# Residual input and final output of a two-layer trunk turned by VectorE's 32x32 transposes and by the transfers, with matmul tiles of every second column

## The chip, the cores and the metric

The kernel runs on one core of a Trainium2 chip. The metric is the device time of one execution in microseconds (us); the figure for the kernel before is the median of its runs. Inputs and outputs are in DRAM, so every load and store counts.

## The reference

One inference step of two layers on 1024 prompt tokens and 8 single decode tokens, in fp32, feature width 1024. What matters here is how the residual runs through it:

```python
def retention_layer(x, S0, g_norm, w_in, g_out, w_out):
    h = rmsnorm(x, g_norm)
    proj = h @ w_in                      # q, k, v, gate
    ...
    o, S = retention_scan(q, k, v, S0)   # 4 heads, 8 chunks of 128 tokens
    o = rmsnorm(o, g_out) * silu(gate)
    return x + o @ w_out, S              # w_out: 2048 x 1024
```

The second layer has the same frame: `h = rmsnorm(x, g)`, a projection to q, k, v and a gate, attention over a window of 128 tokens (16 query heads, 2 key heads, with sinks) in place of the scan, and `x + o @ w_out` with a 1024 x 1024 `w_out_swa`. The results are `y_prompt`, `y_sample` and the new states and caches.

## The kernel before, in words

All activations between the layers lie with features on the 128 partitions and tokens along the free dimension: 1032 token columns, in which columns 1024 to 1031 are the decode tokens. A matrix product takes 128 features of the output at a time, as a PSUM tile of 128 features by up to 512 tokens. Every fp32 operand is split into a high and a low part, so that each product of a 128-row weight block is three matmuls: high times high, high times low, low times high.

The input x and the output y lie in DRAM the other way, with tokens as rows. So x, as it is loaded for the residual, has to be turned, and so has y before it is stored. Before, TensorE does this: `tr` (L100, L101 in the profile) is a matmul against the identity.

The work around the change, in order of time:

- **The scan** (up to about 695 us). It computes the retention. During its last steps the first output tile of `w_out_ret` is already worked on: `b_w` (L1026) loads 128 columns of the weight in four pieces on SP's queue, `b_wc` (L1032) splits them on ScalarE (L1039) and VectorE (L1040), `b_x` (L1043) loads the matching piece of x, `b_wmm` (L1047) multiplies (L1055 to L1057), and four transposes (L1107, L1108) add the residual into the same PSUM tile, named S. In these steps the loads lie in a ring of buffers named evp, evx, evc, evw.
- **The output projection of the retention layer**, called ro here (about 695 to 835 us). It goes by output tiles (ft, gi): ft is one of 8 blocks of 128 features, gi one of the token ranges RG = 0 to 512, 512 to 768, 768 to 1032. First all eight ft of gi 0, then for every ft the ranges gi 1 and 2. The weights come in slots (`wslot`, L1137): 1024 rows by 256 columns, loaded in two halves of 512 KB (L1144, SP's queue, tile wr with two buffers), and split by ScalarE (L1147, tile wh) and VectorE (L1148, tile wl) with the gain of the norm; a slot therefore serves the two neighbouring ft. `ro_ahead` (L1189) issues slots in advance. `ro_part` (L1197) holds the matmuls L1214 to L1216. `ro_xr` (L1222) loads the x of one tile (L1226, L1229). `ro_finish` (L1231) closes a tile: TensorE's transposes add the residual in PSUM (L1241, L1243, in the profile L101 `pj<-ident,xr`), ScalarE copies the sum out (L1250) and writes the next layer's operands from PSUM (L1252), VectorE their low part (L1253), ScalarE squares (L1258), and the sum goes to the DRAM buffer xscr (L1260, ScalarE's queue). At the border of the scan and ro the order is written out (L1281 to L1285): `ro_ahead(2)`, `ro_finish(0, 0)`, then `ro_xr` of the next two tiles.
- **The second layer's projections and attention** (about 835 to 1225 us), with weights of `w_in_swa` through the same `wslot`.
- **The output projection of the second layer**, called so here (its last part runs alone to the end). `so_all` (L1788) goes over tiles (ft, ti), ti one of the token ranges 0 to 384, 384 to 768, 768 to 1032; VectorE adds the residual from xscr (L1813, tile sq), and `so_y` (L1771), one tile late, turns the sum with three transposes (L1777, L1779, in the profile L101 `tr<-ident,sq`), ScalarE copies it out of PSUM (L1781, L1785) and issues the stores (L1782, L1786). The last two feature blocks (ft 6 and 7) stand at the end, ft by ft. Slots of `w_out_swa` are split in blocks of 128x512 (L1154 on ScalarE, L1157 on VectorE). Between the tiles of this last part the decode tokens' attention is finished: L1725 puts its probabilities on a block diagonal, L1737 and L1739 multiply with the values.

In the scan, and where `manual_schedule` stands, each engine's instructions are in the order of the code; elsewhere a scheduler orders them. SP and ScalarE issue their DMAs in order: an issue that has to wait holds back all that stands behind it on its queue.

Of the kernel before, what the change touches and what calls it, by code (L numbers as in the profile page):

```python
# [20 lines left out]
DV = 512  # L21
# [49 lines left out]
def _trunk(ctx, tc, nc, a):  # L71
# [334 lines left out]
    gl = sp.tile([25, 128], F32, name="gl")  # L406
    rT = sp.tile([128, 7, 4, 4], F32, name="rT")
# [213 lines left out]
    def gains():  # L621
        pg = vdp.tile([128, 512], F32, tag="vd", name="pg")
        tr(pg[:, :25], gl, ident[:25, :25])
        heads[0]["pg"] = pg

    def small_loads():
        for o_, src in ((gl[0:16], ret_out_norm.rearrange("o (k p) -> (o k) p", p=128)),
                        (gl[16:24], norm_swa.rearrange("o (k p) -> (o k) p", p=128)),
                        (gl[24:25, 0:64], q_norm), (gl[24:25, 64:128], q_norm)):
            nc.scalar.dma_start(out=o_, in_=src)  # L630
    later(5, small_loads)
    later(14, gains)
    later(15, lambda: act(gcol, heads[0].pop("pg")[:, :25], AF.Copy))
# [392 lines left out]
    def b_w(i):  # L1026

        t = ring("px"[i // 2])[:, 0:512].rearrange("p (k f) -> p k f", k=4)
        nc.sync.dma_start(out=t, in_=w_out_ret[i * 512:i * 512 + 512, 0:128].rearrange("(k p) f -> p k f", p=128))
        wo[i] = t  # L1030

    def b_wc(i):  # L1032

        raw = wo[i]
        hi, lo = [(woh[i + 2 * (x == "l")] if i < 2 else rp.tile([128, DV], F32R, tag="v" + x, name="wo" + x, bufs=2))
                  .rearrange("p (k f) -> p k f", k=4) for x in "hl"]
        for k in range(4):
            gk = gcol[:, 4 * i + k:4 * i + k + 1]
            act(hi[:, k], raw[:, k], AF.Copy, scale=gk)  # L1039
            dve.scalar_tensor_tensor(lo[:, k], raw[:, k], gk, hi.bitcast(F32)[:, k], MUL, SUB)  # L1040
        wo[i] = hi, lo

    def b_x():  # L1043
        wo["x"] = ring("c")[:, 0:512].rearrange("p (c f) -> p c f", c=4)
        nc.sync.dma_start(out=wo["x"], in_=x_prompt[0, 0:512, 0:128].rearrange("(c p) f -> p c f", p=128))

    def b_wmm(i):  # L1047
# [3 lines left out]
        hi, lo = wo[i]  # L1051
        xh, xl, _ = o_view(0)
        for k in range(4):
# [3 lines left out]
            mm(wo["ps"], lo[:, k, :], xh[:, kt, 0:512], start=False, stop=False)  # L1057
# [20 lines left out]
    for i in range(-1, NS + 2):  # L1078
# [8 lines left out]
        if i in (NS - 3, NS - 2):  # L1087
            b_w(i - NS + 3)
        if i in (NS - 2, NS - 1):
            b_w(i - NS + 4)  # L1090
        if i == NS - 1:
            b_x()
# [911 lines left out]
```

## Time and profile before

| | us |
|---|---|
| median of 3 runs | 1313.86 |
| the runs | 1311.10 to 1314.79 |
| the profiled execution | 1314.25 |
| its span, first to last instruction | 1312.2 |
| TensorE (PE) busy | 1284.0 (98%) |
| VectorE (DVE) busy | 727.7 (55%) |
| ScalarE (ACT) busy | 691.4 (53%) |
| GpSimd (POOL) busy | 630.8 (48%) |

The transfers move 193.98 MB in 199907 packets, and the granted TensorE clock is 0.995 of full speed on average. A row of the timeline reads: start in us, duration in us, engine, line, operation, out<-in, shape, count, and in brackets the idle time before it with what ended it. PE's matmuls overlap in a pipeline, so what one costs is read from the distance between starts, not from its duration. SPq and ACTq are DMA issues on the queues of SyncE and ScalarE. In the grouped rows stand, behind the bar, busy time and mean duration in ns, then idle time ahead of the group with its releasers; in the rows of waits, the time in all, how often, and the longest. A row of windows gives, for a stretch of time, each engine's busy time, the granted clock, the DMA engines' busy share and GB/s.

### The profile page before, as it was taken

How to read it: one execution, taken by the hardware profiler on the slowest of the kernel's cores; microseconds unless marked ns; L12 is line 12 of the kernel's file. 1: busy time of each engine (PE TensorE's matmuls, PEld its weight loads, DVE VectorE, ACT ScalarE, POOL GpSimd, SP SyncE). 2: the span in 40 equal slices, each digit the busy share in tenths (PEclk: the TensorE clock that was granted, in tenths of full speed). 3: DMA queues.
4: the chain of work that ended last, by engine and by line, in shares of the span. 5: the costliest groups of instructions: out<-in, count | busy, mean ns of one | idle time of the engine just before them, and what ended most of it. 6: DMA issues, size and time to landing. Idle time of an engine off the chain costs nothing.

```text
span 1312.2 us, 26102 instructions
## 1 busy us (share of the span) xinstructions
PE 1284.0 (98%) x9597; PEld 1212.2 (92%) x9597; DVE 727.7 (55%) x1476; ACT 691.4 (53%) x1722; POOL 630.8 (48%) x800
## 2 busy tenths in 40 slices
PE   6999999999999999999999999999999999999998
PEld 6999999999999999887887889999999999998998
DVE  6944556565565564477785333324665666766321
ACT  5533544554555653577775444445576666666121
POOL 6654544545445544599980110137476676554000
PEclk9999999999999999999999999999998999999999
DMA  6314767677676854456556554353032211237232
GB/s 225 104 61 129 238 197 244 180 234 220 197 239 184 247 174 138 132 169 213 177 165 193 162 165 123 122 147 85 17 106 72 65 58 44 75 110 251 73 96 78
DMA packets 199907, 193.98 MB, mean 148 GB/s; under 512 B 12916, under 2 KB 180140, under 8 KB 199764
## 3 DMA queue, kind: packets, MB, share of 16 engines
q1 hardware_dynamic: 165024, 157.78, 39.2%
q10 hardware_dynamic: 34756, 34.53, 8.3%
q8 instruction: 76, 1.25, 0.4%
q14 instruction: 51, 0.42, 0.1%
HBM read 132.23 MB, written 61.08 MB: 147 GB/s over the span
## 4 chain that ended last, share of the span: by engine, by line
PE 91%; DVE 2%; ACT 2%; DMA 2%; POOL 2%; issue 1%; ACTq 0%; SPq 0%; POOLq 0%; DVEq 0%
PE b L331 7%; PE b L332 7%; PE b L333 7%; PE pj L1167 6%; PE pj L1168 6%; PE pj L1169 6%; PE tr L101 4%; PE b L324 4%; PE b L325 4%; PE b L326 4%; PE pj L1214 4%; PE pj L1215 4%; PE pj L1216 4%; PE o L1645 2%; PE b L538 2%; PE sc L1610 1%
## 5 line engine op out<-in xcount | busy, mean ns | idle before, releaser
L331 PE MATMUL b<-xh,woh 128*128 128x258 f32 x784 | 223.2, 285 | 0.0
L333 PE MATMUL b<-xh,wol 128*128 128x258 f32 x784 | 221.7, 283 | 0.0
L332 PE MATMUL b<-xl,woh 128*128 128x258 f32 x784 | 221.6, 283 | 0.0
L1167 PE MATMUL pj<-A_hi,wh 128*128 128x384 f32 (+1 forms) x512 | 174.9, 342 | 1.7 <-ACT A_hi L1670 1.3
L1168 PE MATMUL pj<-A_lo,wh 128*128 128x384 f32 (+1 forms) x512 | 165.2, 323 | 0.1
L1169 PE MATMUL pj<-A_hi,wl 128*128 128x384 f32 (+1 forms) x512 | 165.1, 322 | 0.0
L331 PEld LDWEIGHTS b<-xh,woh 128*128 128x128 f32 x784 | 148.0, 189 | 4.1 <-issue 3.7
L332 PEld LDWEIGHTS b<-xl,woh 128*128 128x128 f32 x784 | 148.7, 190 | 0.0
L333 PEld LDWEIGHTS b<-xh,wol 128*128 128x128 f32 x784 | 148.0, 189 | 0.0
L222 POOL TENSOR_TENSOR wol<-raw,woh 128x512 fp32r<-128x512 f32 x52 | 68.1, 1318 | 130.9 <-ACT woh L217 128.8
L324 PE MATMUL b<-woh,xh 128*128 128x256 f32 x448 | 126.6, 283 | 0.0
L325 PE MATMUL b<-wol,xh 128*128 128x256 f32 x448 | 126.0, 281 | 0.0
L326 PE MATMUL b<-woh,xl 128*128 128x256 f32 x448 | 125.6, 280 | 0.0
L1167 PEld LDWEIGHTS pj<-A_hi,wh 128*128 128x128 f32 x512 | 97.3, 190 | 5.4 <-issue 2.6
L1168 PEld LDWEIGHTS pj<-A_lo,wh 128*128 128x128 f32 x512 | 97.5, 190 | 0.4 <-DVE A_lo L1671 0.4
L1169 PEld LDWEIGHTS pj<-A_hi,wl 128*128 128x128 f32 x512 | 96.9, 189 | 0.0
L1148 DVE SCALAR_TENSOR_TENSOR wl<-wr,gcol,wh 128x256 fp32r<-128x256 f32 x128 | 53.8, 486 | 68.2 <-ACT wh L1147 68.2
L1259 POOL TENSOR_TENSOR acc<-acc,sq 128x256 f32<-128x256 f32 (+1 forms) x28 | 20.6, 742 | 146.4 <-ACT sq L1258 146.3
L1625 POOL TENSOR_TENSOR s<-s,sm 128x512 f32<-128x512 f32 x64 | 66.5, 1039 | 47.7 <-DVE sm L1624 43.5
L324 PEld LDWEIGHTS b<-woh,xh 128*128 128x128 f32 x448 | 84.3, 188 | 5.0 <-issue 2.9
L326 PEld LDWEIGHTS b<-woh,xl 128*128 128x128 f32 x448 | 84.3, 188 | 0.0
L325 PEld LDWEIGHTS b<-wol,xh 128*128 128x128 f32 x448 | 84.3, 188 | 0.0
(391 smaller groups left out, 3636.6 us busy)
## 6 DMA issues: line engine op xcount, KB each, us to landing
raw<-in_w_in_ret_dram ACTq DMA_DIRECT2D x44, 512.0 KB
st<-in_state_ret_dram SPq DMA_DIRECT2D x64, 256.0 KB
out_dram<-st SPq DMA_DIRECT2D x64, 256.0 KB
wr<-in_w_out_ret_dram SPq DMA_DIRECT2D x32, 512.0 KB
wr<-in_w_in_swa_dram SPq DMA_DIRECT2D x18, 512.0 KB
vb<-vscr SPq DMA_DIRECT2D x64, 128.0 KB
evp<-qks SPq DMA_DIRECT2D x32, 256.0 KB
evx<-vsc SPq DMA_DIRECT2D x32, 256.0 KB
```

The lines of the kernel that those rows point to most:

```text
L222: eng.tensor_tensor(lo, src_of(s, name, sub), hi.bitcast(F32), SUB)
L324: mm(dst, xh, wh, start=a and i == 0, stop=False, skip_group_check=True)
L325: mm(dst, xh, wl, start=False, stop=False, skip_group_check=True)
L326: mm(dst, xl, wh, start=False, stop=z, skip_group_check=True)
L331: mm(dst, wh, xh, start=a, stop=False, **sg)
L332: mm(dst, wh, xl, start=False, stop=False, **sg)
L333: mm(dst, wl, xh, start=False, stop=z, **sg)
L1148: nc.vector.scalar_tensor_tensor(lo[:, k, :], raw[:, k % 4, :], gk, hi.bitcast(F32)[:, k, :], ALU.mult, ALU.subtract)
L1167: mm(ps, hi[:, k, fs], xh[:, k, t0:t1], start=first and k == ks[0], stop=False)
L1168: mm(ps, hi[:, k, fs], xl[:, k, t0:t1], start=False, stop=False)
L1169: mm(ps, lo[:, k, fs], xh[:, k, t0:t1], start=False, stop=last and k == ks[-1])
L1625: nc.gpsimd.tensor_tensor(st[:, :, 0:256], st[:, :, 0:256], sm.unsqueeze(2).broadcast_to([128, 2, 256]), ALU.mult)
```

## The change

TensorE no longer turns the residual or the output. VectorE has a transpose that turns each 32x32 block of a tile in its place; the transfers put the blocks where they belong. A block row of 32 partitions then holds, in DRAM, runs of 64 features (256 bytes) of one token, so that a load of x for 256 features and 256 tokens is four DMAs of 32 partitions. Since such a tile carries 64 features in a row for each group of 32 partitions, a matmul tile takes every second column of a block of 256: the even ones are ft = 2p, the odd ones 2p + 1. All that depends on the order of features follows: the slots of both output weights are split with a stride of two columns, the rows of `w_in_swa` are loaded in pairs (`rows_load`, two DMAs of 256 KB for one of 512 KB), and the gain of the second norm is turned in the new order (`gs`, two small transposes on TensorE early in the kernel).

- In ro, `ro_finish` takes a VectorE transpose of the loaded x and a VectorE addition of PSUM and x in place of the PE transposes and the ScalarE copy; the operations behind it read SBUF, not PSUM. The decode tokens' x is loaded and turned once (`ro_xd`).
- In the scan, `b_x` and its four transposes are gone; `b_w` loads 256 rows by 256 columns in eight pieces and uses every second column.
- At the border of scan and ro, `ro_xr` for the first two pieces (eight DMAs) now stands ahead of `ro_ahead(2)`.
- In so, `so_y` is a VectorE transpose into a tile that two neighbouring ft share; after the second of them four DMAs store it (four more for the decode tokens). The two last ft go range by range, so that pairs end together. Slots of `w_out_swa` are split in eight blocks of 128x256.

The core of the diff:

```diff
-    def b_w(i):
-        t = ring("px"[i // 2])[:, 0:512].rearrange("p (k f) -> p k f", k=4)
-        nc.sync.dma_start(out=t, in_=w_out_ret[i * 512:i * 512 + 512, 0:128].rearrange("(k p) f -> p k f", p=128))
+    def b_w(i, tag):
+        wo[i] = ring(tag)[:, 0:512].rearrange("p (k f) -> p k f", k=2)
+        nc.sync.dma_start(out=wo[i], in_=w_out_ret[i * 256:i * 256 + 256, 0:256].rearrange("(k p) f -> p k f", p=128))
...
-        for n in {NS - 2: (0,), NS - 1: (1, 2), NS: (3,)}.get(i, ()):
+        for n in {NS - 2: (0,), NS - 1: (1, 4, 2, 3, 5), NS: (6, 7)}.get(i, ()):
             b_wc(n)
...
-    for i in range(4):
-        tr(wo["ps"][:, i * 128:i * 128 + 128], wo["x"][:, i, :], ident, start=False, stop=(i == 3))
...
-    def wslot(src, gain=None):
+    def wslot(src, gain=None, out=False):
...
+                h2, l2 = [t[:, k, :].rearrange("p (u q) -> p u q", u=2) for t in (hi, lo)]
+                r2 = raw[:, k % 4, :].rearrange("p (q u) -> p u q", u=2)
+                if gain is not None:
+                    gk = gcol[:, gain + k:gain + k + 1]
+                    nc.scalar.activation(h2, r2, AF.Copy, scale=gk)
+                    nc.vector.scalar_tensor_tensor(l2, r2, gk, h2.bitcast(F32), ALU.mult, ALU.subtract)
+                else:
+                    nc.scalar.activation(h2, r2, AF.Copy)
+                    lo_eng[0].tensor_tensor(l2, r2, h2.bitcast(F32), ALU.subtract)
...
+    def ro_xr(pr, a):
+        xr = ro_x[pr, a] = fp.tile([128, 8, 64], F32, name="xr", bufs=4)
+        v = x_prompt[0, a:a + 256, 256 * pr:256 * pr + 256].rearrange("(a i) (b f) -> b i a f", i=32, b=4)
+        for b in range(4):
+            nc.sync.dma_start(out=xr[32 * b:32 * b + 32], in_=v[b])
...
-            for i in range(nfull):
-                tr(ps[:, i * 128:i * 128 + 128], xr[:, i, :], ident, start=False, stop=(i == nfull - 1))
...
-            nc.scalar.activation(x1[:, :n], pv, AF.Copy)
+            nc.vector.transpose(x1[:, 0:256], xr[:, u])
+            nc.vector.tensor_tensor(x1[:, 0:256], ps[:, a - t0:a - t0 + 256], x1[:, 0:256], ALU.add)
...
     with tc.manual_schedule(engines={ET.Activation, ET.DVE, ET.Pool, ET.SP}):
+        for a_ in (0, 256):
+            ro_xr(0, a_)
         ro_ahead(2)
         ro_finish(0, 0)
-        for ft in (1, 2):
-            ro_xr(ft, 0)
+        ro_xd()
...
-        for i in range(nch):
-            tr(pt[:, i * 128:i * 128 + 128], yt[:, i * 128:i * 128 + 128], ident)
...
+        nc.vector.transpose(yo[:, 0:nb, :, u], yt[:, 0:32 * nb])
+        if u == 1:
+            fs = slice(256 * pr, 256 * pr + 256)
+            v = y_p[0, t0:t0 + npr, fs].rearrange("(a i) (b f) -> b i a f", i=32, b=4)
+            for b in range(4):
+                bs = slice(32 * b, 32 * b + 32)
+                nc.scalar.dma_start(out=v[b], in_=yo[bs, 0:na].rearrange("i a j u -> i a (j u)"))
```

What follows is the order of the instructions on two engines where the prediction speaks of them; it holds no times.

SP's queue at the border of the scan and ro, before. Tiles evp, evx, evc are the ring in which the scan's last loads lie (L1029 are the four loads of `b_w`, L1045 the load of `b_x`), wr are halves of weight slots.

```order
L1029 DMA evp<-in_w_out_ret_dram 128x4x128
L1029 DMA evx<-in_w_out_ret_dram 128x4x128 x2
L1045 DMA evc<-in_x_prompt_dram 128x4x128
L1144 DMA wr<-in_w_out_ret_dram 128x4x256 x4
L1226 DMA xr<-in_x_prompt_dram 128x4x128 x2
```

The same place after (L1038 are the last of the eight loads of `b_w`, L1240 the decode tokens' x).

```order
L1038 DMA evx<-in_w_out_ret_dram 128x2x256
L1038 DMA evc<-in_w_out_ret_dram 128x2x256
L1038 DMA evp<-in_w_out_ret_dram 128x2x256
L1038 DMA evw<-in_w_out_ret_dram 128x2x256
L1249 DMA xr<-in_x_prompt_dram 32x8x64 x8
L1149 DMA wr<-in_w_out_ret_dram 128x4x256 x2
L1249 DMA xr<-in_x_prompt_dram 32x8x64 x2
L1149 DMA wr<-in_w_out_ret_dram 128x4x256 x2
L1240 DMA xd<-in_x_sample_dram 8x4x64 x4
```

The loads of x, which stood behind the first four halves of weight slots, now stand ahead of them.

VectorE in so, where the decode tokens' probabilities are put on their diagonal (L1725), before; tiles sq are the sums with the residual.

```order
L1813 TENSOR_TENSOR sq_15986<-pj_15961,xr2_15959 128x384
L1813 TENSOR_TENSOR sq_16022<-pm_15997,xr2_15995 128x384
L1725 TENSOR_TENSOR pm8_16055<-tr_16056,ident_70 8x128
L1813 TENSOR_TENSOR sq_16071<-pj_16033,xr2_16031 128x384
L1813 TENSOR_TENSOR sq_16124<-pj_16082,xr2_16080 128x384
L1745 TENSOR_TENSOR gdec_78<-gdec_78 128x64
```

The same place after (L1836 are the sums, L1799 the transposes of the output, L1743 is the former L1725).

```order
L1836 TENSOR_TENSOR sq_16052<-pm_16027,xr2_16025 128x384
L1799 STREAM_TRANSPOSE yo_16101<-sq_16052 128x384
L1836 TENSOR_TENSOR sq_16099<-pj_16061,xr2_16059 128x384
L1799 STREAM_TRANSPOSE yo_16101<-sq_16099 128x384
L1836 TENSOR_TENSOR sq_16147<-pj_16105,xr2_16103 128x384
L1743 TENSOR_TENSOR pm8_16083<-tr_16084,ident_70 8x128
L1799 STREAM_TRANSPOSE yo_16183<-sq_16147 128x384
L1763 TENSOR_TENSOR gdec_78<-gdec_78 128x64
```

Before, two sums stood between the diagonal and what is done with the decode tokens' attention (L1745, now L1763); now the diagonal stands behind both.

VectorE in so, where the low parts wl of the last slot of `w_out_swa` (ft 6 and 7) are made, before; the sums with 264 columns are those of the tokens 768 to 1032, of ft 0 to 5.

```order
L1813 TENSOR_TENSOR sq_16196<-pj_16171,xr2_16169 128x264
L1813 TENSOR_TENSOR sq_16232<-pj_16207,xr2_16205 128x264
L1157 TENSOR_TENSOR wl_16396<-wr_16397,wh_16395 128x512 x2
L1157 TENSOR_TENSOR wl_16396<-wr_16403,wh_16395 128x512
L1813 TENSOR_TENSOR sq_16270<-pm_16245,xr2_16243 128x264
L1157 TENSOR_TENSOR wl_16396<-wr_16403,wh_16395 128x512
```

The same place after (L1161 is the former L1157).

```order
L1836 TENSOR_TENSOR sq_16350<-pj_16325,xr2_16323 128x264
L1799 STREAM_TRANSPOSE yo_16392<-sq_16350 128x288
L1836 TENSOR_TENSOR sq_16389<-pm_16364,xr2_16362 128x264
L1799 STREAM_TRANSPOSE yo_16392<-sq_16389 128x288
L1161 TENSOR_TENSOR wl_16395<-wr_16396,wh_16394 128x256 x4
L1161 TENSOR_TENSOR wl_16395<-wr_16406,wh_16394 128x256 x4
L1836 TENSOR_TENSOR sq_16443<-pj_16418,xr2_16416 128x384
```

The low parts have moved from behind the second and third of these sums to behind the sixth and its transpose, directly ahead of the first sum that uses them.

132 lines of the change are left out of this document (68 added, 64 removed).

## The prediction

> **What bounds the kernel now.** I read the page's busy times first, then its chain.
>
> ```profile
> PE 1284.0 (98%) x9597; PEld 1212.2 (92%) x9597; DVE 727.7 (55%) x1476; ACT 691.4 (53%) x1722; POOL 630.8 (48%) x800
> PE 91%; DVE 2%; ACT 2%; DMA 2%; POOL 2%; issue 1%; ACTq 0%; SPq 0%; POOLq 0%; DVEq 0%
> ```
>
> TensorE is busy for 98% of the span and holds 91% of the chain; VectorE and ScalarE have nearly half their time free. So an instruction taken off PE is worth its place in PE's row of starts, and work added to VectorE or ScalarE is worth nothing unless PE waits for it. Next I read the stages around the change by windows.
>
> ```profile
> 700.00:712.00 12.00, 12.00 (x54) 9.23 (x53) 6.29 (x16) 8.38 (x21) 0.00 (x0) 1.00 0.83 252
> 712.00:724.00 12.00, 11.26 (x50) 8.26 (x49) 6.52 (x16) 7.33 (x19) 1.44 (x2) 1.00 0.70 218
> 780.00:834.00 54.00, 54.00 (x450) 53.37 (x449) 20.08 (x47) 25.20 (x65) 6.96 (x9) 1.00 0.45 139
> 1256.00:1262.00 6.00, 6.00 (x32) 6.00 (x32) 0.65 (x3) 1.25 (x5) 0.00 (x0) 0.72 0.45 143
> ```
>
> In ro PE has no idle time except 0.74 us between 712 and 724, at the head, where the DMA engines are at 0.70 to 0.83. Later (780 to 834) VectorE works 20 of 54 us and ScalarE 25.
>
> **What goes from PE.** The price of a group of transposes is read from starts: the distance between the undisturbed matmuls on either side, less the usual pace. From PE's timeline, a tile of gi 0:
>
> ```profile
> 720.50 0.39 PE L1216 MATMUL pj<-A_hi,wl 128*128 128x512 f32 x1
> 720.73 0.60 PE L101 MATMUL pj<-ident,xr 128*128 128x128 f32 x4
> 721.09 0.48 PE L1214 MATMUL pj<-A_hi,wh 128*128 128x512 f32 x1
> 721.40 0.40 PE L1215 MATMUL pj<-A_lo,wh 128*128 128x512 f32 x1
> 721.64 0.40 PE L1216 MATMUL pj<-A_hi,wl 128*128 128x512 f32 x1
> ```
>
> Of gi 1, of gi 2, and of so:
>
> ```profile
> 809.18 0.28 PE L1216 MATMUL pj<-B_hi,wl 128*128 128x256 f32 x1
> 809.30 0.38 PE L101 MATMUL pj<-ident,xr 128*128 128x128 f32 x2
> ...
> 809.65 0.29 PE L1215 MATMUL pj<-B_lo,wh 128*128 128x264 f32 x1
> 809.77 0.29 PE L1216 MATMUL pj<-B_hi,wl 128*128 128x264 f32 x1
> ```
>
> ```profile
> 802.97 0.28 PE L1216 MATMUL pj<-B_hi,wl 128*128 128x264 f32 x1
> 803.18 0.59 PE L101 MATMUL pj<-ident,xr 8*128 8x8 f32 x3
> ...
> 803.73 0.28 PE L1215 MATMUL pj<-B_lo,wh 128*128 128x256 f32 x1
> ```
>
> ```profile
> 1286.77 0.34 PE L1168 MATMUL pj<-A_lo,wh 128*128 128x384 f32 x1
> 1286.95 0.33 PE L1169 MATMUL pj<-A_hi,wl 128*128 128x384 f32 x1
> 1287.12 0.49 PE L101 MATMUL tr<-ident,sq 128*128 128x128 f32 x3
> ...
> 1287.62 0.34 PE L1168 MATMUL pj<-A_lo,wh 128*128 128x384 f32 x1
> ```
>
> In gi 0 there are 0.90 us from 720.50 to 721.40, where two steps of 0.235 would stand: 0.43 for four transposes, seven times (ft 1 to 7), 3.0 us. In gi 1: 0.47 less two steps of 0.12, so 0.23, eight times, 1.8. In gi 2: 0.76 less 0.24, so 0.52, eight times, 4.2. In so: 0.67 less two steps of 0.175, so 0.32, for 23 groups 7.4; the 24th lies in the tail. Together 16.4 us. Two small transposes of the gain are added early, about 0.2. I take 16.2.
>
> **What the head of ro loses.** Here the change moves loads, so SP's, PE's and ScalarE's rows count.
>
> ```profile
> 688.67 11.15 SPq L1144 DMA_DIRECT2D wr<-in_w_out_ret_dram  x4
> 694.73 0.39 PE L1057 MATMUL S<-A_hi,wol 128*128 128x512 f32 x1
> 694.96 0.60 PE L101 MATMUL S<-ident,evc 128*128 128x128 f32 x4
> 695.59 3.31 ACT L1147 ACTIVATE wh<-wr,gcol 128x256 fp32r<-128x256 f32 x8 [4.61 <-PE S L101]
> 696.16 0.51 PE L1214 MATMUL pj<-A_hi,wh 128*128 128x512 f32 x1 [0.60 <-ACT wh L1147]
> ```
>
> Before, the first two weight halves are issued at 688.67, long ahead of need, and PE stands still for only 0.60. After, SP's queue has eight loads of x ahead of them. Their tiles lie in memory that the scan's weights hold until its last matmul (694.73, done about 695.1); SP waits there, and the weights, which could go at 688.67, wait behind. The issue pace is in this row, the landing in two pieces of the chain.
>
> ```profile
> 699.98 0.94 SPq L1226 DMA_DIRECT2D xr<-in_x_prompt_dram  x2
> ```
>
> ```profile
> 699.45 4.52 DMA wr<-in_w_out_ret_dram
> 706.25 3.94 DMA wr<-in_w_out_ret_dram
> ```
>
> One issue takes 0.47, eight 3.8. With the scan's end 0.5 us later (its splits are in ten pieces on VectorE at the end, where there were eight; I bound this by -1 and +1), the weights are issued at about 699.4. A half lands 3.9 to 4.5 us later when two share the engines; for the first of a pair I estimate 3.1 (2.7 to 4.5). The first split adds 0.52: PE starts at about 703.1 in place of 696.16, 7.0 later. The 0.74 of idle time that PE had between 712 and 724 is covered then: 6.3. What is unknown is the clock after seven idle microseconds. The window at 1256 shows it at 0.72 over 6 us, after a stretch in which PE had only small matmuls, so 1.7 us lost; from 0 to 1.7, I take 1.0. Head: 7.3.
>
> The Trainium skill, TensorE: Matmul & The Clock Gate, Part 1 (The HAM clock gate), has the clock at half after an idle window of about 3.4 us, and back after as long a busy one. By it an estimated 1.7 us would be lost for certain, and the sum would be 0.7 worse.
>
> The eight loads are packets of 256 bytes, of which the trace has hardly any. The queue's row gives a price for about 1 KB:
>
> ```profile
> q1 hardware_dynamic: 165024, 157.78, 39.2%
> ```
>
> That is 0.392 x 16 x 1312.2 us over 165024 packets, 50 ns for 956 bytes. 2048 packets on 16 engines are 128 each: 1.7 us if the price goes with the bytes, 6.4 us if every packet costs 50 ns. The first is hidden behind 3.8 us of issuing, the second adds 2.6. I take none, since some price between is likelier. The head's bounds are 5.2 (start of issue at once, landing 2.7, clock kept: 5.9 - 0.7) and 13 (scan 0.5 later still, landing 4.5, 1.7 of clock, 2.6 of packets).
>
> **What so loses.** Two waits of PE are new, both from VectorE's order.
>
> ```profile
> 1254.54 0.34 PE L1169 MATMUL pj<-A_hi,wl 128*128 128x384 f32 x1
> 1254.81 0.48 PE L1737 MATMUL o<-pm,vdd 8*128 8x128 f32 x2
> 1254.92 0.56 DVE L1813 TENSOR_TENSOR sq<-pj,xr 128x384 f32<-128x384 f32 x1 [3.98 <-PE pj L1169]
> ```
>
> L1737 needs the diagonal of L1725. That operation (0.28 us) ran at 1249.95; it now stands behind the sum of the very tile that PE finishes at 1254.54. So PE waits until 1254.92 + 0.56 + 0.28 and two handovers, about 1255.85: 1.0, and between 0, if that sum is of an earlier tile, and 1.3.
>
> Before the first tile of ft 6 VectorE must now finish the last sum (0.43, from the tail's row below), its transpose and the first low part.
>
> ```profile
> L1148 DVE SCALAR_TENSOR_TENSOR wl<-wr,gcol,wh 128x256 fp32r<-128x256 f32 x128 | 53.8, 486 | 68.2 <-ACT wh L1147 68.2
> L1157 DVE TENSOR_TENSOR wl<-wr,wh 128x512 fp32r<-128x512 f32 x16 | 12.0, 776 | 3.4 <-ACT wh L1154 3.3
> PE pj L1167 <- ACT A_hi L1670: 1.3, 1, 1.3
> ```
>
> A split piece of 128x256 takes 0.49. No row shows a VectorE transpose; between 0.25 and 1.0, I take 0.40, near the sum of the same shape. From the last matmul's start 0.32 + 0.43 + 0.40 + 0.49 and handovers, 1.8; PE can do two matmuls meanwhile, about 0.5 with the step: a wait of 1.3, bounds 0.8 to 1.9. The later pieces at 0.49 keep ahead of PE's three matmuls (0.53). The other slots of `w_out_swa` cost VectorE 8 x 0.49 for 4 x 0.78, 0.8 more each, and ScalarE as much, during attention, where PE's longest wait for ScalarE is the 1.3 above: 0.4 for all, from 0 to 1.3.
>
> **The tail.**
>
> ```profile
> 1307.06 0.28 PE L1169 MATMUL pm<-A_hi,wl 128*128 128x264 f32 x1
> 1307.38 0.43 DVE L1813 TENSOR_TENSOR sq<-pm,xr 128x264 f32<-128x264 f32 x1 [2.67 <-PE pm L1169]
> 1309.60 0.32 ACTq L1786 DMA_DIRECT2D out_dram<-yo  x1
> ```
>
> From the last sum (done 1307.81) to the last issue go 1.8 us now. After: a transpose 0.4, handover 0.1, and eight issues, of which the last starts 7 x 0.46 = 3.2 later, 3.7 in all: 1.8 lost (1.2 to 2.5).
>
> Free, I think: in ro VectorE gains 32 transposes and ScalarE loses 32 copies, against 34 us free of 54; the halved loads of `w_in_swa` (two issues for one) cost SP half a microsecond each, and it mostly waits. If that cover were gone, a late slot would show as PE waiting for wh.
>
> **Sum.** 16.2 - 7.3 - 1.0 - 1.3 - 0.4 - 1.8 = 4.4 us. The profiled execution took 1314.25, so 1309.85; the median lies 0.39 lower: 1309.5. The sum of the kindest ends is 16.2 - 5.2 - 0.8 - 1.2 = 9.0, of the worst 16.2 - 13 - 1.3 - 1.9 - 1.3 - 2.5 = -3.8: 1304.9 to 1317.7.
>
> **Rivals.** *The head is hidden.* If the loads of x don't hold the weights back (their memory comes free before the last matmul), only 0 to 1 us is lost and the kernel gains about 11: 1303. For it: the DMA engines have room. Against: SP's order, and that the x loads need that memory.
>
> *Operations with a stride of two cost more.* All splits of output weights now read every second fp32, and the transposes too; no row shows such an operation. At twice the price a round of two halves at the head (6.8 us from 699.45 to 706.25) lasts 4 x 0.49 longer, while PE uses a half slot in 24 x 0.235 = 5.6; three rounds lose 5.7, the last slot of so about 2.5 more: 1309.5 + 8.2 = 1317.7. In gi 1 and gi 2 VectorE then needs for two slots 16 x 0.97 + 4 x 1.8 = 22.7 us against PE's 22.8, so beyond twice the price it becomes the bound. From just over 2.0 times it is slower, at 2.2 times about 1324.
>
> *Short packets.* Eight loads at 90 ns a packet take 11.5 us, 7.7 more than their issues: 1317.2, and slower from 95 ns. Against it: that is nearly double the 50 ns of a packet four times as long. The Trainium skill, DMA: Bandwidth & Descriptors, Specifications, states that transfers below 512 bytes miss the line rate through read-modify-write. It names no such price, and no run here shows one.
>
> That the transposes stay on PE can be ruled out: the order of its instructions has them gone.
>
> **Chances.** The forecast's case 0.68, the hidden head 0.13, strides 0.10, packets 0.09. About 0.3% (3.9 us) is what a measurement of this kernel tells from no change: faster means below 1309.9, slower above 1317.8. The forecast's case is divided 0.37 faster, 0.29 same, 0.02 slower; the hidden head is faster; strides 0.02 same and 0.08 slower; packets 0.05 same and 0.04 slower. Faster 0.50, same 0.36, slower 0.14. The range, 1302 to 1316.5, takes in the hidden head with a microsecond to spare and most of the bounds; it leaves out the two cases of high prices.
>
> **What would show it.** Right: PE's first `L1214` near 703 behind SP's eight loads of x, waits for wh there; one wait of about 1 us ahead of the former L1737, one ahead of the first tile of ft 6; no `L101` among the tiles; the last eight issues on ScalarE's queue in a row. Wrong: weight halves landing before 697; PE waiting for wl or for the residual throughout ro; VectorE's splits well above 0.49.

## The result and the profile after

| | before | after |
|---|---|---|
| median, us | 1313.86 (three runs) | 1330.81 (four runs) |
| runs of after, us | | 1329.11 to 1333.10 |
| ratio, with 95% interval | | 1.0135 [1.0108, 1.0161] |
| profiled execution, its span | 1314.25, 1312.2 | 1330.76, 1329.0 |

The kernel became slower by 17.0 us. A fourth execution of the kernel before, in the same series, took 2023.47 us and is left out of the median and the ratio. The forecast was a gain of 4.4 us; its sign was wrong, and the time lies outside its range. First the same two rows of the page of after that the prediction began with.

```profile
PE 1274.6 (96%) x9455; PEld 1204.3 (91%) x9455; DVE 770.7 (58%) x1590; ACT 677.2 (51%) x1675; POOL 633.2 (48%) x809
PE 87%; DVE 4%; DMA 3%; POOL 2%; ACT 2%; issue 1%; SPq 0%; ACTq 0%; POOLq 0%; DVEq 0%
```

PE did lose work: 142 matmuls and 9.4 us of busy time. But its share of the chain fell from 91% to 87%: other engines and the transfers now hold PE up. The rows of waits of after say for what.

```profile
PE pj L1226 <- ACT wh L1157: 8.3, 1, 8.3
...
PE pj L1179 <- ACT wh L1160: 5.9, 1, 5.9
...
PE pm L1537 <- ACT sq L1516: 3.7, 1, 3.7
...
PE S L1061 <- ACT woh L1050: 1.6, 1, 1.6
```

The first is the wait at the head of ro that was forecast, the second is one ahead of the last slot that was not (5.9 us for ScalarE). The windows of after show the head, the middle of ro, and the end of so.

```profile
700.00:712.00 12.00, 5.52 (x13) 4.36 (x14) 3.50 (x8) 4.01 (x9) 0.00 (x0) 0.58 0.65 189
...
780.00:834.00 54.00, 54.00 (x407) 51.80 (x406) 26.54 (x65) 22.74 (x52) 6.57 (x9) 1.00 0.53 143
1262.00:1300.00 38.00, 31.22 (x212) 30.59 (x211) 11.13 (x29) 3.52 (x12) 0.71 (x6) 0.90 0.41 92
```

Between 700 and 712 PE is busy for 5.52 us at a clock of 0.58, where before it was busy for all 12 at 1.00. In the middle of ro (780 to 834) it is as full as before, with VectorE at 26.5 of 54 us. At the end of so (1262 to 1300) it stands idle for 6.8 us.

**Where the time went.** I set each matmul that both kernels have against itself: the start after, less the start before. For PE's first matmul of ro that is 706.48 - 696.16 = 10.32. The differences of this shift from place to place sum to the difference of the spans, 16.8 (16.9 as rounded here).

| place | forecast | measured |
|---|---|---|
| transposes out of ro; out of so | -9.0; -7.4 | -8.6; -6.9 |
| small transposes of the gain | +0.2 | +0.2 |
| end of the scan | +0.5 | +2.9 |
| loads of x ahead of the weights | +6.5 | +7.2 |
| half clock behind that wait | +1.0 | +2.6 |
| the next slots of ro | -0.7 | +1.9 |
| attention | +0.4 | +7.0 |
| the diagonal, `dec_o` | +1.0 | +1.0 |
| last slot of `w_out_swa` | +1.3 | +8.2 |
| tail | +1.8 | +1.4 |

So the gain came as forecast, and five of the costs didn't. The rows of after for four of them follow, in order of time; those of the attention stand at e7.

*End of the scan.* ScalarE's splits of the pieces, from the timeline, and a row of waits of SP's queue:

```profile
684.63 0.71 ACT L1050 ACTIVATE woh<-evp,gcol 128x128 fp32r<-128x128 f32 x2 [2.44 <-DMA evp<-in_w_out_ret_dram]
...
688.01 0.70 ACT L1050 ACTIVATE woh<-evp,gcol 128x128 fp32r<-128x128 f32 x2 [2.67 <-DMA evp<-in_w_out_ret_dram]
```

```profile
SPq L1038 <- POOL ql L821: 9.2, 3, 3.7
```

SP has to hold three of the eight issues back (9.2 us in all), because the ring tiles into which they load are still read by GpSimd. ScalarE, in order, waits 2.44 and 2.67 us for two of the late pieces (the third and fourth in its list), and the norm of the last chunk stands behind them; PE waits 1.6 us for the split weights and 1.9 for the norm.

*Head of ro.* SP's queue, then PE:

```profile
698.30 3.80 SPq L1249 DMA_DIRECT2D xr<-in_x_prompt_dram  x8
702.15 1.00 SPq L1149 DMA_DIRECT2D wr<-in_w_out_ret_dram  x2
```

```profile
697.84 0.39 PE L1063 MATMUL S<-A_hi,wol 128*128 128x512 f32 x1
706.48 0.79 PE L1226 MATMUL pj<-A_hi,wh 128*128 128x512 f32 x1 [8.26 <-ACT wh L1157]
707.07 0.63 PE L1227 MATMUL pj<-A_lo,wh 128*128 128x512 f32 x1
707.50 0.63 PE L1228 MATMUL pj<-A_hi,wl 128*128 128x512 f32 x1
```

The loads of x start when the scan's last matmul is done, eight issues take 3.80 us, and PE starts 4.33 us after the first weight issue (3.6 were forecast): step by step the mechanism of the forecast. Then matmuls of 512 columns come 0.43 us apart instead of 0.235, until 712.2.

*The next slots of ro.* VectorE, and PE behind it:

```profile
720.51 0.45 DVE L1264 STREAM_TRANSPOSE x<-xr 128x256 f32<-128x256 f32 x1 [1.28 <-DMA xscr<-x]
720.88 2.82 DVE L1158 SCALAR_TENSOR_TENSOR wl<-wr,gcol,wh 128x256 fp32r<-128x256 f32 x7
```

```profile
DVE x L1264 <- DMA xscr<-x: 21.1, 13, 3.8
```

```profile
729.50 0.80 PE L1228 MATMUL pj<-A_hi,wl 128*128 128x512 f32 x1 [1.86 <-DVE wl L1158]
...
732.23 0.63 PE L1228 MATMUL pj<-A_hi,wl 128*128 128x512 f32 x1
732.66 0.44 PE L1226 MATMUL pj<-A_hi,wh 128*128 128x512 f32 x1
```

VectorE's transpose writes a tile of two buffers that the store to xscr must first have left. It waits for such stores 13 times, 21.1 us in all, and the splits wl stand behind it. Once PE feels it: 1.86 us, and again about 1.4 of half clock. That VectorE has free time (26.5 of 54 us) says nothing of this: a part of that free time is waiting.

*Last slot.* ScalarE's queue ahead of the split, and PE:

```profile
1283.95 7.72 ACTq L1809 DMA_DIRECT2D out_dram<-yo  x4
...
1295.43 1.42 ACTq L1809 DMA_DIRECT2D out_dram<-yo  x4
1296.90 0.43 ACT L1160 ACTIVATE wh<-wr 128x256 fp32r<-128x256 f32 x1 [27.78 <-DMA out_dram<-yo]
```

```profile
1297.38 0.69 PE L1179 MATMUL pj<-A_hi,wh 128*128 128x384 f32 x1 [5.86 <-ACT wh L1160]
```

Four of the small stores of decode tokens take 7.72 us here, where four took 1.42 at 1295.43. The order of the instructions says what an issue waits for. The last of these stores and the split, in order:

```
L1805 DMA out_dram<-yo 32x8x64 [waits DMAHW2_49,DVE_49]
L1805 DMA out_dram<-yo 32x8x64 [waits DMAHW3_49]
L1805 DMA out_dram<-yo 32x8x64 [waits DMAHW4_49]
L1805 DMA out_dram<-yo 32x8x64 [waits DMAHW5_49]
L1809 DMA out_dram<-yo 8x64 [waits DMAHW6_49]
L1809 DMA out_dram<-yo 8x64 [waits DMAHW7_49]
L1809 DMA out_dram<-yo 8x64 [waits DMAHW0_49]
L1809 DMA out_dram<-yo 8x64 [waits DMAHW1_49]
L1160 ACTIVATE wh<-wr 128x256 [waits PE_49]
```

The transfers of SP's and ScalarE's queues signal their ends, in this program, on eight semaphores, DMAHW0 to 7, taken in turn; an issue waits until the transfer that had the same semaphore before it is done. That earlier transfer can be one of the other queue: a load of the residual (L1820) on SP, which itself waits for VectorE.

```profile
1283.33 6.12 SPq L1820 DMA_DIRECT2D xr<-xscr  x3
```

```profile
SPq L1820 <- DVE sq L1836: 75.8, 19, 8.0
```

The second and third of these three loads are issued at 1286.23 and 1289.13; the small stores that wait for the same two semaphores are issued at 1288.62 and 1291.39, 2.4 and 2.3 us later. So a split on ScalarE stands behind sixteen stores from 1281 on (and five before), some of these behind loads of SP, and those behind VectorE's sums.

### The profile page after: what moved, and what is told of

The parts are those of the page before. It is cut to its first block, busy times and chain, and to the rows that moved or that the text cites. A ratio compares the mean times of both kernels' runs of the same rounds, so it can differ in the third digit from the quotient of the medians.

```text
span 1329.0 us, 25969 instructions
## 1 busy us (share of the span) xinstructions
PE 1274.6 (96%) x9455; PEld 1204.3 (91%) x9455; DVE 770.7 (58%) x1590; ACT 677.2 (51%) x1675; POOL 633.2 (48%) x809
## 4 chain that ended last, share of the span: by engine, by line
PE 87%; DVE 4%; DMA 3%; POOL 2%; ACT 2%; issue 1%; SPq 0%; ACTq 0%; POOLq 0%; DVEq 0%
PE b L331 7%; PE b L332 7%; PE b L333 7%; PE pj L1179 6%; PE pj L1180 5%; PE pj L1181 5%; PE b L324 4%; PE b L325 4%; PE b L326 4%; PE pj L1228 4%; PE pj L1226 4%; PE pj L1227 4%; PE tr L101 3%; PE o L1663 2%; PE b L539 2%
## 5 line engine op out<-in xcount | busy, mean ns | idle before, releaser
L1276 POOL TENSOR_TENSOR acc<-acc,sq 128x256 f32<-128x256 f32 (+1 forms) x28 | 21.1, 759 | 146.1 <-ACT sq L1275 146.0
L1635 ACT ACTIVATE s<-s,mx 128x257 f32<-128x257 f32 x128 | 64.2, 505 | 36.7 <-DVE mx L1633 36.3
```

The lines of the kernel that those rows point to most:

```text
L1635: nc.scalar.activation(st[:, j, :], st[:, j, :], AF.Exp, bias=mx[:, j:j + 1], accum_out=sm[:, j:j + 1])
```

## The experiments

The theory drawn from these rows (T): the gain on PE is real and is given back at four places on in-order queues, each of which can be mended by itself: SP's order at the head, the pieces at the scan's end, the store that VectorE waits for, the stores ahead of the last split, and besides by finer splits during attention. The rivals were the prediction's (strides that cost more; short packets), and that the new stages are as slow as they are for VectorE's order. Each ratio is against the kernel before on the same chip. Beside it stands what the trace of the experiment shows against after, by the same count of shifts, at the place of the edit: scan is from 660 us to the scan's last matmul, head from there to 750 us, and all is from 660 us to the end.

| kernel | median, us | ratio [95%] | at its place, us |
|---|---|---|---|
| after | 1330.81 | 1.0135 [1.0108, 1.0161] | |
| e1, first slot ahead of x | 1323.35 | 1.0074 [1.0058, 1.0089] | head -7.6 |
| e2, pieces in another order | 1325.87 | 1.0094 [1.0076, 1.0112] | scan -3.9 |
| e3, last split early | 1321.18 | 1.0061 [1.0046, 1.0076] | last slot -8.55 |
| e4, fewer stores | 1323.92 | 1.0075 [1.0056, 1.0095] | last slot -7.2 |
| e5, x1 in four buffers | 1327.78 | 1.0099 [1.0079, 1.0118] | head -3.2 |
| e6, two slots ahead, x1 in four | 1322.60 | 1.0063 [1.0045, 1.0080] | head -7.6 |
| e7, splits of 512 | 1322.46 | 1.0060 [1.0040, 1.0081] | attention -4.65 |
| e8, e2 to e7 together | 1306.24 | 0.9935 [0.9916, 0.9954] | all -22.7 |
| e9, e8 with fewer loads of x | 1306.66 | 0.9951 [0.9936, 0.9966] | head -8.7 (e8: -8.0) |
| e10, e9 with the tail on two queues | 1305.12 | 0.9942 [0.9923, 0.9961] | |
| e11, before with x first | 1319.54 | 1.0049 [1.0033, 1.0064] | head +9.1 on before |
| e12, e10 with xd on GpSimd's queue | 1302.42 | 0.9927 [0.9906, 0.9947] | head -12.2, all -29.8 |

The head also moves in runs whose edit lies elsewhere: by -0.3 in e3, -0.6 in e2, -1.5 in e4 and -2.6 in e7. So a shift there of less than about 3 us proves nothing by itself.

**e1: the first weight slot ahead of the loads of x.**

```diff
+        ro_ahead(1)
         for a_ in (0, 256):
             ro_xr(0, a_)
         ro_ahead(2)
```

> The changed kernel with the first weight slot of ro issued ahead of the eight loads of x, the second behind them; nothing else differs. The theory of queue order (the weights stood behind loads that wait for the scan's last matmul): the first weight halves go about 691 in place of 702.2, PE's first matmul of ro starts near 698.5 in place of 706.5, the stretch at half clock behind it goes, and the kernel gains about 10 us: 1321. The theory of short packets (the loads of x are slow because their packets have 256 bytes, and hold up whatever comes next): the third and fourth half then arrive late in place of the first, and no more than 4 us are gained: 1327 or more.

The time, 1323.35, is nearer to T's 1321 than to the rival's 1327 or more, but 2.4 us short of T. SP's queue of e1, and then PE's waits that are left:

```profile
692.03 0.92 SPq L1149 DMA_DIRECT2D wr<-in_w_out_ret_dram  x2
696.57 3.81 SPq L1249 DMA_DIRECT2D xr<-in_x_prompt_dram  x8
```

```profile
704.65 0.50 PE L1226 MATMUL pj<-A_hi,wh 128*128 128x512 f32 x1 [2.56 <-ACT wh L1157]
...
714.57 0.49 PE L1228 MATMUL pj<-A_hi,wl 128*128 128x512 f32 x1 [2.42 <-DVE wl L1158]
```

The weights go out 4.5 us before the loads of x, which still wait for their tiles, and the wait of 8.3 us is gone. The same eight loads now hold back the second slot (2.56), and the store of x1 the low part (2.42).

**e2: the pieces of the scan's end.**

```diff
-{NS - 3: ((0, "p"),), NS - 2: ((1, "p"), (4, "x")), NS - 1: ((2, "p"), (5, "x"), (6, "c"), (3, "p")),
+{NS - 3: ((0, "p"),), NS - 2: ((1, "p"), (2, "x")), NS - 1: ((3, "x"), (4, "c"), (5, "p"), (6, "p")),
...
-{NS - 2: (0,), NS - 1: (1, 4, 2, 3, 5), NS: (6, 7)}
+{NS - 2: (0,), NS - 1: (1, 2, 3), NS: (4, 5, 6, 7)}
```

> The changed kernel with the eight weight pieces of the scan's last steps renumbered, so that those loaded early are used early, and with the splits of the last four moved behind the next step's norm. The theory of order (ScalarE waited 2.4 and 2.7 us for pieces that SP issued late, and the norm stood behind them): PE's waits of 1.6 and 1.9 us at 688 and 692 go, ro starts 2.5 to 3.5 us earlier, 1327.5. The rival (eight loads in place of four are too many for the last steps, in whatever order): the same waits at another piece, less than 1 us gained.

With the splits in the order in which the pieces can come, the whole shift of the scan's end goes (-3.9 against +2.9), and the time with it (1325.87 for 1327.5 expected). So it was not the number of splits, as the forecast had it, which is the same in e2, but the loads that two of them waited for ahead of the norm. The edit both renumbers the pieces and moves two splits behind the norm; which of the two did more isn't shown.

**e3 and e4: the last slot.** e3 issues the split of the last slot earlier, ahead of the stores; e4 leaves it where it is and stores the decode tokens' output once at the end, not with every pair.

```diff
-            so_ahead(ft // 2 + 1)
+            so_ahead(4 if ti == 2 and ft >= 2 else ft // 2 + 1)
```

> The changed kernel with the last slot of w_out_swa asked for two tiles of the last token range earlier (at ft 2 in place of ft 6); nothing else differs. The theory of queue order (the split stands behind 16 stores on ScalarE): PE's wait of 5.9 us for wh ahead of ft 6 goes, with the stretch at half clock behind it: about 8 us, 1323. The rival (the slot's load itself comes late, or VectorE is late with the low parts): PE still waits 1 us or more there, and less than 5 us are gained.

```diff
+        ysall = acc[:, 0:256].rearrange("p (q j u) -> p q j u", q=4, u=2)
+        if ti == 2:
+            nc.vector.transpose(ysall[:, pr, :, u], yt[:, 256:288])
...
-            if ti == 2:
-                v = y_s[:, 0, fs].rearrange("i (b f) -> b i f", b=4)
+            if ti == 2 and pr == 3:
+                v = y_s[:, 0, :].rearrange("i (q b f) -> b i q f", q=4, b=4)
                 for b in range(4):
-                    nc.scalar.dma_start(out=v[b], in_=yo[32 * b:32 * b + 8, na].rearrange("i j u -> i (j u)"))
+                    nc.scalar.dma_start(out=v[b], in_=ysall[32 * b:32 * b + 8].rearrange("i q j u -> i q (j u)"))
```

> The changed kernel with the decode tokens' output collected in SBUF and stored by four DMAs at the end, in place of four for each pair (12 small DMAs fewer; VectorE has one small transpose more for each tile of the last range). The split of the last slot keeps its place behind the stores of the prompt tokens. The theory of shared semaphores (a DMA's issue waits for an earlier DMA of either queue, here for SP's loads of the residual, which wait for VectorE): without the 8 small issues ahead of it the split starts at about 1288 in place of 1296.9 (in time of the changed kernel), PE's wait for wh falls from 5.9 to 1.5 us or less, and 4.5 to 7 us are gained: 1325. The rival (the stores are slow because of their 256-byte packets): the stores of y_p, which stay, hold the split just as long less 8 short issues, 2 us gained at most.

The split of e3 on ScalarE, and PE's wait for it in e4:

```profile
1278.21 1.42 ACT L1160 ACTIVATE wh<-wr 128x256 fp32r<-128x256 f32 x4 [10.73 <-DMA out_dram<-yo]
```

```profile
PE pj L1179 <- ACT wh L1160: 0.7, 1, 0.7
```

Either edit takes the 8.2 us away almost whole, and both times are a little better than expected (1323 and 1325). With e4 the rival of 256-byte stores, 2 us at most, is out. e4 is the sharper of the two, since it leaves VectorE's order ahead of the slot as it is, but for six small transposes more, and takes only stores from ScalarE's queue: the wait falls from 5.9 to 0.7. The forecast's 1.3 us for VectorE's order is not what was paid.

**e5 and e6: x1 and the slots.** e5 gives x1 four buffers; e6 does so too and puts both slots of `ro_ahead(2)` ahead of the loads of x.

```diff
-            x1 = fp.tile([128, 264], F32, name="x1", bufs=2)
+            x1 = fp.tile([128, 264], F32, name="x1", bufs=4)
```

> The changed kernel with four buffers in place of two for x1, the tile into which VectorE turns the residual and from which xscr is stored. The theory of the blocked queue (VectorE's transpose waits for the store of the x1 before last, and the splits behind it on VectorE wait too): VectorE's waits for xscr (21.1 us in all) go, and with them PE's wait of 1.9 us for wl at the head of ro; 1.5 to 2.6 us gained, 1328.5. The rival (the head is paced by the landing of the weights): PE waits for wh in place of wl, nothing gained.

```diff
+        ro_ahead(2)
         for a_ in (0, 256):
             ro_xr(0, a_)
-        ro_ahead(2)
```

> The changed kernel with both weight slots of ro issued ahead of the loads of x, as in the kernel before, and four buffers for x1. Both theories of the head together: what is left of the head's loss is the scan's end (3 us), PE's waits between 696 and 724 fall under 1 us, half clock goes; against the kernel with only the first slot ahead (1323) the second slot's wait of 2.6 us and the wl wait of 2.4 us go: 1319. If the short packets of x are the limit, VectorE waits for xr ahead of its first transpose and the splits behind it are late: 1322 or more.

VectorE's waits for xscr and PE's for wl in e5:

```profile
DVE x L1264 <- DMA xscr<-x: 8.6, 4, 4.0
```

```profile
PE pj L1228 <- DVE wl L1158: 0.4, 1, 0.4
```

e5 is as expected in time, but its interval overlaps that of after, so it is the waits that count. Of VectorE's 21.1 us for xscr 8.6 are left, none of them between 690 and 760. PE's wait for wl at the head is 0.7 to 2.4 us in the six traces of after, e1 to e4 and e7, with two buffers, and 0.4 or not seen in e5, e6, e8 and e12, with four. So the store that VectorE waited for was the cause of the +1.9. e6 missed by 3.6 us; it was to gain what e1 and e5 gain together and is no better than e1. SP's queue and PE in e6:

```profile
701.77 5.40 SPq L1249 DMA_DIRECT2D xr<-in_x_prompt_dram  x8
707.27 3.00 SPq L1240 DMA_DIRECT2D xd<-in_x_sample_dram  x4
710.39 0.95 SPq L1149 DMA_DIRECT2D wr<-in_w_out_ret_dram  x2
```

```profile
715.17 0.70 PE L1226 MATMUL pj<-A_hi,wh 128*128 128x512 f32 x1 [5.12 <-ACT wh L1157]
```

The twelve issues now stand ahead of the third slot, and PE waits there instead. The order at the head moves a part of the cost along the queue. That the source of this part is the twelve issues that x now takes is tested by e9 and e12.

**e7: splits of `w_out_swa` in blocks of 512 again, the stride of two kept.**

```diff
-            for k in range(4 * j, 4 * j + 4) if out else ():
+            for k in range(4 * j, 4 * j + 4, 2) if out and gain is None else ():
+                h2, l2 = [t[:, k:k + 2, :].rearrange("p k (u q) -> p k u q", u=2) for t in (hi, lo)]
+                r2 = raw[:, k % 4:k % 4 + 2, :].rearrange("p k (q u) -> p k u q", u=2)
...
```

> The changed kernel with the slots of w_out_swa split in four blocks of 128x512 (two row blocks at a time, still by every second column) in place of eight of 128x256, as large as in the kernel before. If the 4.0 us that the changed kernel loses at the end of the attention (1199 to 1206 in time of before) come from the longer splits on ScalarE and VectorE, 2 to 4 us are gained: 1328. If they come from the order in which the scheduler puts the attention's last steps, nothing or either sign by less than 1.5 us.

Better than expected by 5.5 us. At its place the trace shows 4.65. Of after's +7.0 in the attention, 4.9 lie there (1193 to 1206 in time of before): PE waits three times for VectorE and ScalarE, where before it had one wait of 1.28 us, and a stretch at half clock follows (the granted clock of after is 0.86 from 1208 to 1220). PE in after:

```profile
1202.52 0.39 PE L1628 MATMUL sc<-kkh,qs 128*128 128x256 f32 x1 [1.31 <-DVE s L1631]
...
1211.96 0.44 PE L1179 MATMUL pj<-A_hi,wh 128*128 128x384 f32 x1 [2.67 <-ACT A_hi L1688]
1213.53 0.44 PE L1180 MATMUL pj<-A_lo,wh 128*128 128x384 f32 x1 [1.13 <-DVE A_lo L1689]
```

In e7 the first is down to 0.33 us, the last two have become the one of before, and the clock is 1.00:

```profile
1204.65 0.45 PE L1180 MATMUL pj<-A_hi,wh 128*128 128x384 f32 x1 [1.28 <-ACT A_hi L1689]
```

The rest lies elsewhere (-2.6 in the head, ahead of the edit, and -1.5 in so, where the clock of after is 0.86 from 1262 to 1274 and that of e7 1.00 from 1250 to 1262), and I can't put it down to the edit: the clock also differs where nothing was changed, as the last section shows. In e8, e9, e10 and e12, which have the edit too, its place shows -4.5 to -4.7. So the finer splits hurt where ScalarE and VectorE are the tightest, in the attention, not in so.

**e8 to e10: all together, and fewer loads.** e8 has the edits of e2, e3, e4, e6 and e7.

> The changed kernel with all repairs: slots ahead of the loads of x, four buffers for x1, scan pieces renumbered, the last slot's split early, decode output stored at the end, splits of 128x512. If the losses are separate waits they add up: 11 (head with x1) + 3.5 (scan) + 8.5 (last slot) + 2 (splits), 25 us less than the changed kernel, 1306, and faster than the kernel before by 7, which is the transposes' 16 us less the tail, the diagonal and the attention's rest. If they share one cause (the short packets, or one queue whose waits only move), less than 18 us: 1313 or more, no better than before.

As expected, and faster than before: the four places and the splits hold most of the loss. e9 loads x for 512 tokens with four DMAs, not eight, and issues the decode tokens' x (xd) on ScalarE's queue; e10 sends half of the last pair's stores on SP's.

```diff
-            nc.sync.dma_start(out=xd[32 * b:32 * b + 8], in_=v[b])
+            nc.scalar.dma_start(out=xd[32 * b:32 * b + 8], in_=v[b])
```

> The kernel with all repairs, and the loads of x joined: four DMAs for 512 tokens in place of eight, the same packets of 256 bytes; the decode tokens' x is loaded on ScalarE's queue. The theory of issues (SP's queue is taken up by 12 issues between the second and third weight slot, 8.4 us, and PE waits 4.1 us for the third slot): the third slot's halves go 4 to 6 us earlier, the wait falls under 1.5 us and the half clock behind it goes, 3 to 6 us gained: 1302. The rival of short packets: the same number of packets takes the same time, PE's wait stays over 3 us, less than 1.5 us gained.

```diff
-                nc.scalar.dma_start(out=v[b], in_=yo[bs, 0:na]
+                (nc.sync if pr == 3 and b % 2 else nc.scalar).dma_start(out=v[b], in_=yo[bs, 0:na]
```

> As the joined one, with half of the last pair's output stores on SP's queue. The tail's eight issues on one queue cost about 3.2 us after the last transpose; with two of them on the other queue about 0.8 us are gained, 1301 if joining gives 1302; if the stores wait for their packets and not for their issue, nothing.

e9 missed: no faster than e8. ScalarE's first split of the third slot in e9, and PE:

```profile
709.88 0.52 ACT L1161 ACTIVATE wh<-wr,gcol 128x256 fp32r<-128x256 f32 x1 [3.08 <-DMA xd<-in_x_sample_dram]
```

```profile
710.46 0.79 PE L1227 MATMUL pj<-A_hi,wh 128*128 128x512 f32 x1 [2.84 <-ACT wh L1161]
```

The four issues of xd, moved from SP to ScalarE, held up ScalarE's split for 3.08 us: the mistake of after's last slot once more. So the time is that of the rival of short packets, but what PE waits for is not the loads of x; e12 tests it. e10 can't be told from e9, so that edit is inconclusive.

**e11: the order alone, in the kernel before.** Its two loads of x (128 partitions, 512-byte packets, two issues) ahead of `ro_ahead(2)`, nothing else.

```diff
+        for ft in (1, 2):
+            ro_xr(ft, 0)
         ro_ahead(2)
         ro_finish(0, 0)
-        for ft in (1, 2):
-            ro_xr(ft, 0)
```

> The kernel before, with its two loads of x (packets of 512 bytes, two issues) ahead of the first two weight slots of ro, nothing else. The theory of queue order: the weights go at 696.1 in place of 688.7 (0.9 us of issues behind the scan's last matmul at 695.1), PE's first matmul of ro comes near 700.4 in place of 696.2, and 3.5 to 6 us are lost, with the half clock if the idle time is enough for it: 1318. The rival of short packets: with long packets and only two issues the order costs less than 2 us: 1315.

SP's queue, PE and the window of e11:

```profile
693.71 0.92 SPq L1226 DMA_DIRECT2D xr<-in_x_prompt_dram  x2
694.67 20.47 SPq L1144 DMA_DIRECT2D wr<-in_w_out_ret_dram  x7
```

```profile
701.11 0.79 PE L1214 MATMUL pj<-A_hi,wh 128*128 128x512 f32 x1 [7.04 <-ACT wh L1147]
```

```profile
700.00:712.00 12.00, 10.89 (x35) 8.71 (x36) 6.65 (x16) 8.20 (x20) 0.00 (x0) 0.70 0.47 146
```

Without one short packet, two issues ahead of the weights cost 9.1 us of shift, 6.4 of wait and 2.7 of half clock, against 9.8 (7.2 and 2.6) in after with eight issues. That is more than the 3.5 to 6 expected, and by the medians 6.3; the trace of e11 lacks an earlier 1.6 us of half clock that those of before and after have. So standing behind the wait for the tiles of x costs nearly all of it, with two issues as with eight, and the size of the packets need not be called upon. Only the sum is shown to be alike: e11's two issues take 0.9 us, but PE starts 6.4 us after the first weight issue, where after needs 4.33.

**e12: e10 with xd on GpSimd's queue**, which neither the weights nor the splits use.

```diff
-            nc.sync.dma_start(out=xd[32 * b:32 * b + 8], in_=v[b])
+            nc.gpsimd.dma_start(out=xd[32 * b:32 * b + 8], in_=v[b])
```

> As the one with two queues for the tail, with the four loads of the decode tokens' x on GpSimd's queue, which has nothing to do there, in place of ScalarE's. The theory of issues: ScalarE's split of the third slot waited 3.1 us for these four loads (their issues took 3.0 us on its queue), and PE 2.8 us for the split; both go, with the half clock behind: 3 to 4 us gained, 1302. The rival (at that point the weights' landing is the limit): PE waits for wh as long as before, nothing gained, 1305.

The head's window of e12, and its row of waits for wh:

```profile
700.00:712.00 12.00, 10.77 (x44) 7.83 (x44) 8.71 (x23) 6.69 (x16) 1.61 (x2) 1.00 0.99 222
```

```profile
PE pj L1227 <- ACT wh L1161: 1.7, 2, 1.1
```

At the head PE's clock is 1.00 and its waits for wh have shrunk from 8.3 to 1.7 us. e12 takes 0.7% less than before [0.5, 0.9], where after took 1.4% more. Its time, 1302.42, is the 1302 expected, but whether it beats e8 to e10 the intervals don't tell; that the wait at the head is gone is read from the trace.

## Why the prediction was wrong

Between the forecast (-4.4) and the trace (+16.8) lie 21.2 us. Five terms of the sum account for 20.1: the last slot (6.9), the attention (6.6), the next slots of ro (2.6), the end of the scan (2.4) and the half clock at the head (1.6).

- **What goes from PE: right.** 15.5 us measured for 16.4; the price of a group, read from the starts around it, was good to 6%.
- **The head: right in the mechanism, too low in size.** The step "the clock ... from 0 to 1.7, I take 1.0" is a term that was mis-sized: half clock lasted from 706.5 to 712.2 and cost 2.6 us. The Trainium skill, TensorE: Matmul & The Clock Gate, Part 1 (The HAM clock gate), which I set beside it, was nearer with half clock for certain. But its idle window of about 3.4 us is not needed: after the wait of 1.86 us at 729.50 the matmuls also come 0.43 us apart, until 732.66.
- **The end of the scan: wrong.** I counted VectorE's splits (ten for eight, 0.5 us). I didn't follow the loads: each of the eight needs a ring tile that comes free at a time of its own, and two of the splits ahead of the norm were of late ones. e2 shows it.
- **"Free, I think: in ro VectorE gains 32 transposes ... against 34 us free of 54": wrong, by 2.6 us** (+1.9 for -0.7). VectorE did have the time (26.5 us busy of 54). The transpose brought a wait for a buffer, and the splits stand behind it in order. e5 shows it.
- **"0.4 for all, from 0 to 1.3" for the slots during attention: wrong, +7.0.** I bounded it by PE's longest wait for ScalarE before. Of the 7.0, 4.9 lie between 1193 and 1206, and e7, with the coarser splits, takes 4.65 of them away, in waits and half clock. The rest is +1.1 at 907 to 917 and +0.9 net at about 990 (where PE's wait for the squares has grown from 2.1 to 3.7 us). I tested neither; their cause stays open.
- **The last slot: the wrong engine.** The step priced VectorE's order (1.3 us). The split of ScalarE behind sixteen stores wasn't considered: in the kernel before, stores were few and late. 8.2 us, the largest miss; e3 and e4 show it.
- **The diagonal and the tail: right,** 1.0 for 1.0 and 1.4 for 1.8.
- **The rivals.** The head was not hidden. Strides cost nothing: the grouped rows of after have VectorE's split at 488 ns, where 486 stood before.

```profile
L1158 DVE SCALAR_TENSOR_TENSOR wl<-wr,gcol,wh 128x256 fp32r<-128x256 f32 x128 | 54.9, 488 | 32.0 <-ACT wh L1157 31.9
L1264 DVE STREAM_TRANSPOSE x<-xr 128x256 f32<-128x256 f32 x32 | 14.1, 441 | 26.5 <-DMA xscr<-x 21.1 <-DMA xr<-in_x_prompt_dram 5.1 <-DVE wl L1158 0.2
```

  The transpose, taken at 0.40 us, took 0.44. Nor did short packets decide, by e11.

The failure is one of kind: the waits that I followed step by step (the head but for its clock, the diagonal, the tail) were priced well, and the losses that the experiments explain lie where a DMA or an operation was added to an in-order queue ahead of something that PE needs. I had asked that question of SP at the head alone.

## What to carry to other kernels

Moving work from the engine that bounds to engines with free time is worth its PE time only if nothing PE waits for stands behind it: list, for every queue that gains an instruction, what that instruction can wait for and which split or load comes next behind it. Count DMAs as instructions of a queue, not as bytes: four for one cost issue time, and they wait for each other. Where such a change comes out slower, its queues can be mended one at a time, and the fall of PE's busy time (9.4 us here, with the half clock in it) says that there is something to win.

## What the hardware showed beside

- **Two queues wait for each other.** In this program, issues of ScalarE wait for transfers of SP through the eight semaphores: four stores of 8x64 numbers took 7.72 us to issue at 1283.95 and 1.42 at 1295.43.
- **A short packet takes less time, though more by the byte.** Between 1262 and 1329 ScalarE's queue moved 11008 packets of 242 bytes on average:

```profile
q10 hardware_dynamic: 11008, 2.66, 22.4%
q1 hardware_dynamic: 2400, 2.59, 14.2%
```

  0.224 x 16 x 67 us over 11008 is 22 ns each, against 63 ns for 1079 bytes on SP's (0.142 x 16 x 67 us over 2400). That is 11 against 17 bytes a nanosecond, of stores against loads. The Trainium skill, DMA: Bandwidth & Descriptors, Specifications, asks for at least 512 bytes for line rate; these numbers agree in the direction.
- **The same wait costs differently from one execution to the next.** One stretch of the scan, which no edit touches, in after and in e1:

```profile
500.00:560.00 60.00, 56.91 (x406) 53.50 (x405) 27.57 (x62) 27.00 (x64) 28.00 (x43) 0.97 0.40 127
```

```profile
500.00:560.00 60.00, 56.91 (x417) 53.52 (x416) 29.01 (x65) 28.22 (x66) 29.62 (x45) 1.00 0.44 136
```

  PE is idle for the same 3.09 us, and the clock is 0.97 in the one and 1.00 in the other: 1.6 us of span. That is why the shifts of the experiments are not counted from the start.
